# Router softmax on one core: fewer filler matmuls late, late copies out of PSUM shared with ScalarE, the last row loaded in two pieces, and the first store held back

## The chip, the cores and the metric

The kernel runs on one core of one Trainium2 chip. The metric is the device time of one execution in microseconds (us). The kernel before takes 91.72 us, the median of three runs (91.64 to 91.76). The profiled execution took 91.54 us, and its trace spans 89.8 us; the times of the trace count from the start of that span.

## The reference

```python
x: (16, 512, 1024) float32, router_weights: (1024, 8) float32

def reference(x, router_weights):
    logits = np.matmul(x, router_weights)
    exp_logits = np.exp(logits - np.max(logits, axis=-1, keepdims=True))
    return (exp_logits / np.sum(exp_logits, axis=-1, keepdims=True)).astype(np.float32)
```

There are 8192 tokens of 1024 values each. Each is multiplied by a thin 1024x8 matrix, and a softmax over the 8 results follows. The input is 33.6 MB, the output 0.26 MB.

## The kernel before

**Tiling.** Token 64p + j belongs to partition p, so the 8192 tokens are 64 "rows" j of 128 tokens, one for each partition (J = 64). The list `LOADS` says how many rows each transfer brings: thirteen loads of 4 rows, three of 2 and six of 1. The first 4 rows come as float32 on SyncE's queue and are cast by ScalarE (L72). All others are issued by GpSimd (L74), whose queue casts float32 to bfloat16 on the way. All tiles of x stay in SBUF, so no load waits for a buffer of x. GpSimd issues them in order, each from the ninth on after an earlier load has landed.

**A row.** A matmul needs the 1024 values of a token along the partitions, and they lie along the free axis. So TensorE transposes a row in eight 128x128 pieces against an identity matrix into one PSUM tile `pt` (`turn`, L147 to L149; the pool has 4 such tiles[...]). VectorE copies the tile to SBUF as `xT` (L156). Then eight matmuls with 8 columns each accumulate the row's logits (`project`, L98 to L109) into a PSUM tile `lg` of the row's group. The program order on TensorE is written out by hand (a manual schedule): the transposes of row j, then the projection of row j - 2, then fillers.

**Fillers.** `fill(n)` issues n matmuls of 512 columns on constant data into a PSUM tile that nobody reads (L95). They only keep TensorE active. From row 24 to row 61 there are two for each row (L162, L163).

**Softmax.** `GROUPS` puts the rows into seven groups of 8, one of 7 and one of 1. When a group's last row is projected, five steps go into the list `later`: the maximum (`peak`), the subtraction on VectorE and exp on ScalarE (`power`), the sum (`total`), the reciprocal (`recip`), and the scaling into the output tile `outv` (`scale`, L138). The loop over rows pops one step after each row's copy (L157, L158), so they run between the copies on VectorE.

**The end.** The loop covers rows 0 to 62 (L151). After it come the projections of rows 61 and 62 (L166, L167), two softmax steps of the group of 7, and then row 63: four transposes and a copy of 512 columns, twice (L174 to L176), its projection, two more steps, the maximum (L182), an exp that also adds up the row (L185), the last step of the group of 7, a reciprocal (L188) and a scaling (L189). Two stores go out on SyncE's queue: rows 0 to 55 right after group 6 is scaled (L143), and rows 56 to 63 at the very end (L191).

Of the kernel before, what the change touches and what calls it, by code (L numbers as in the profile page):

```python
# [9 lines left out]
@with_exitstack  # L10
def kernel(
    ctx: ExitStack,
    tc: tile.TileContext,
    x: bass.AP,
    router_weights: bass.AP,
    out: bass.AP,
):
    nc = tc.nc
    P = 128
    B, S, D = x.shape  # L20
    D2, N = router_weights.shape
    assert D2 == D
    M = B * S
    KO = D // P
    J = M // P


    x_rows = x.rearrange("b s d -> (b s) d").rearrange("(p j) d -> p j d", p=P)
    out_rows = out.rearrange("b s n -> (b s) n").rearrange("(p j) n -> p j n", p=P)

    fp32 = mybir.dt.float32
    bf16 = mybir.dt.bfloat16
    Exp = mybir.ActivationFunctionType.Exp
    X = mybir.AxisListType.X
    ALU = mybir.AluOpType


    LOADS = [4] * 13 + [2, 2, 2] + [1] * 6
    GROUPS = [8] * 7 + [7, 1]
    assert sum(LOADS) == J and sum(GROUPS) == J  # L40
    STORES = {6: (0, 56), 8: (56, J)}

    const = ctx.enter_context(tc.tile_pool(name="const", bufs=1))
    xpool = ctx.enter_context(tc.tile_pool(name="x", bufs=1))
    xtp = ctx.enter_context(tc.tile_pool(name="xT", bufs=5))
    sm = ctx.enter_context(tc.tile_pool(name="sm", bufs=2))
    psum_t = ctx.enter_context(tc.tile_pool(name="psum_t", bufs=4, space=bass.MemoryType.PSUM))
    psum_f = ctx.enter_context(tc.tile_pool(name="psum_f", bufs=1, space=bass.MemoryType.PSUM))
    psum_l = ctx.enter_context(tc.tile_pool(name="psum_l", bufs=2, space=bass.MemoryType.PSUM))

    x_of = []
    with tc.manual_schedule():
        identity = const.tile([P, P], bf16)
        ident = const.tile([P, P], fp32)
        w8 = const.tile([KO, P, N], fp32)
        w_bf = const.tile([P, KO, N], bf16)
        outv = const.tile([P, J, N], fp32)
        filler = const.tile([P, 512], bf16)


        x_f32 = const.tile([P, LOADS[0], D], fp32)
        for k in range(0, LOADS[0], 2):
            nc.sync.dma_start(out=x_f32[:, k:k + 2, :], in_=x_rows[:, k:k + 2, :])
        nc.scalar.dma_start(
            out=w8[:], in_=router_weights.rearrange("(ko ki) n -> ko ki n", ko=KO)
        )
        j0 = 0
        for i, r in enumerate(LOADS):
            xb = xpool.tile([P, r, D], bf16, name=f"x_{i}", tag=f"x_{i}")
            if i == 0:  # L70
                for k in range(r):
                    nc.scalar.copy(xb[:, k, :], x_f32[:, k, :])  # L72
            else:
                nc.gpsimd.dma_start(out=xb[:], in_=x_rows[:, j0:j0 + r, :])  # L74
            x_of += [(xb, k) for k in range(r)]
            j0 += r
            if i == 2:
                make_identity(nc, ident)
                nc.gpsimd.memset(filler[:], 0.5)  # L79
        nc.vector.tensor_copy(out=identity[:], in_=ident[:])  # L80
        w_ps = psum_l.tile([P, 8, N], fp32, name="lg")
        for n in range(N):
            nc.tensor.transpose(w_ps[:, n, :], w8[:, :, n], ident[0:KO, 0:KO])  # L83
        nc.vector.tensor_copy(out=w_bf[:], in_=w_ps[:].rearrange("p n ko -> p ko n"))  # L84

        group_of = [(g, k) for g, n in enumerate(GROUPS) for k in range(n)]
        first = [sum(GROUPS[:g]) for g in range(len(GROUPS))]
        logits = {}
        pend = []
        later = []  # L90
        spare = psum_f.tile([P, 512], fp32)

        def fill(n):
            for _ in range(n):
                nc.tensor.matmul(spare[:], lhsT=filler[:, 0:P], rhs=filler[:], start=True, stop=True)  # L95


        def project(j, xT):  # L98
            g, k = group_of[j]
            if k == 0:  # L100
                logits[g] = psum_l.tile([P, 8, N], fp32, name="lg")
            for ko in range(KO):
                nc.tensor.matmul(  # L103
                    logits[g][:, k, :],
                    lhsT=xT[:, ko, :],
                    rhs=w_bf[:, ko, :],
                    start=(ko == 0),
                    stop=(ko == KO - 1),
                )  # L109
            if k == GROUPS[g] - 1 and g < len(GROUPS) - 1:  # L110
                softmax(g)

        def softmax(g):
            n, a = GROUPS[g], first[g]
            lg = logits.pop(g)[:, 0:n, :]
            mx = sm.tile([P, n, 1], fp32, name="mx")
            ex = sm.tile([P, n, N], fp32, name="ex")
            ev = sm.tile([P, n, N], fp32, name="ev")
            ssum = sm.tile([P, n, 1], fp32, name="ssum")
            inv = sm.tile([P, n, 1], fp32, name="inv")  # L120

            def peak():
                nc.vector.reduce_max(mx[:, :, 0], lg, axis=X)  # L123

            def power():
                nc.vector.tensor_tensor(  # L126
                    out=ex[:], in0=lg, in1=mx[:].broadcast_to([P, n, N]), op=ALU.subtract
                )
                nc.scalar.activation(ev[:], ex[:], func=Exp)  # L129

            def total():
                nc.vector.reduce_sum(ssum[:, :, 0], ev[:], axis=X)  # L132

            def recip():
                nc.vector.reciprocal(inv[:], ssum[:])  # L135

            def scale():
                nc.vector.tensor_tensor(  # L138
                    out=outv[:, a:a + n, :], in0=ev[:], in1=inv[:].broadcast_to([P, n, N]), op=ALU.mult
                )  # L140
                if g in STORES:
                    lo, hi = STORES[g]
                    nc.sync.dma_start(out=out_rows[:, lo:hi, :], in_=outv[:, lo:hi, :])  # L143

            later.extend([peak, power, total, recip, scale])

        def turn(pt, xb, kos):  # L147
            for ko in kos:
                nc.tensor.transpose(pt[:, ko, :], xb[:, ko * P:(ko + 1) * P], identity[:])  # L149

        for j in range(J - 1):  # L151
            xb, k = x_of[j]
            pt = psum_t.tile([P, KO, P], bf16, name="pt")
            turn(pt, xb[:, k, :], range(KO))
            xT = xtp.tile([P, KO, P], bf16, name="xT")
            nc.vector.tensor_copy(out=xT[:], in_=pt[:])  # L156
            if later:  # L157
                later.pop(0)()  # L158
            pend.append((j, xT))
            if len(pend) > 2:  # L160
                project(*pend.pop(0))
            if 24 <= j < J - 2:  # L162
                fill(2)  # L163


        for p in pend:  # L166
            project(*p)  # L167
        for _ in range(2):
            later.pop(0)()
        xb, k = x_of[J - 1]  # L170
        pt = psum_t.tile([P, KO, P], bf16, name="pt")
        xT = xtp.tile([P, KO, P], bf16, name="xT")
        H = KO // 2
        for kos in (slice(0, H), slice(H, KO)):  # L174
            turn(pt, xb[:, k, :], range(KO)[kos])
            nc.vector.tensor_copy(out=xT[:, kos, :], in_=pt[:, kos, :])  # L176
        project(J - 1, xT)
        for _ in range(2):
            later.pop(0)()
        lg1 = logits.pop(len(GROUPS) - 1)[:, 0, :]  # L180
        low = sm.tile([P, 1], fp32, name="low")
        nc.vector.reduce_max(low[:], lg1, axis=X, negate=True)  # L182
        ev1 = sm.tile([P, N], fp32, name="ev1")
        s1 = sm.tile([P, 1], fp32, name="s1")
        nc.scalar.activation(ev1[:], lg1, func=Exp, bias=low[:], accum_out=s1[:])  # L185
        for step in later:
            step()
        nc.vector.reciprocal(s1[:], s1[:])  # L188
        nc.vector.tensor_scalar_mul(outv[:, J - 1, :], ev1[:], s1[:])  # L189
        lo, hi = STORES[len(GROUPS) - 1]  # L190
        nc.sync.dma_start(out=out_rows[:, lo:hi, :], in_=outv[:, lo:hi, :])  # L191


# [28 lines left out]
```

## Time and profile before

| | before |
|---|---|
| device time, median of 3 | 91.72 us |
| span of the trace | 89.8 us |
| busy: TensorE / VectorE / ScalarE / GpSimd | 65.9 / 50.2 / 7.7 / 12.4 us |
| mean granted TensorE clock | 0.973 of full |
| read from HBM, written | 33.59 MB, 0.26 MB |
| TensorE on transposes (L149) / projections (L103) / fillers (L95) | 43.6 / 22.6 / 22.5 us |
| VectorE on copies out of PSUM (L156) | 43.3 us, 63 copies of 690 ns |
| store of rows 0 to 55: issued, landed after | 84.04 us, 1.9 us |
| store of rows 56 to 63: issued, landed after | 87.42 us, 1.5 us |

The page gives busy time by engine and by group of instructions; the busy times of TensorE's lines overlap, because matmuls are pipelined. The time that a row really takes on TensorE is the distance between the starts of two rows in the timeline. "Landing" is the time from a transfer's issue to the moment at which its completion is seen. Busy shares over the whole span say little here, since the end of the kernel has other limits than its middle; the prediction goes by stretches of the timeline.

### The profile page before, as it was taken

The page shows a single profiled execution, that of the slowest core. Times are in us where ns is not written, and L with a number is a line of the kernel's source. Part 1 is how long each engine was busy: PE and PEld are TensorE (multiplying, and loading weights), DVE is VectorE, ACT ScalarE, POOL GpSimd, SP SyncE. Part 2 cuts the span into 40 slices and gives each one's busy share as a digit, 9 for nine tenths or more (in the row PEclk, how much of TensorE's full clock was granted, in tenths as well). Part 3 has the DMA queues.
Part 4 walks back from the last instruction along what each step waited for, and adds up shares of the span by engine and source line. Part 5 has one row for each costly group of instructions (what it writes and reads, how often), then busy time and mean ns, then how long its engine had stood idle before and what let it go on. Part 6 is the DMA issues. An engine that isn't in the chain of part 4 may idle for free.

```text
span 89.8 us, 2442 instructions
## 1 busy us (share of the span) xinstructions
PE 65.9 (73%) x1108; PEld 54.3 (60%) x1108; DVE 50.2 (56%) x110; ACT 7.7 (9%) x15; POOL 12.4 (14%) x28
## 2 busy tenths in 40 slices
PE   0408008999773819699898989599989999999520
PEld 0406008999663819676775757377757777777410
DVE  0304103669791917657475657457774777677760
ACT  3143035000100010000100010000100010001110
POOL 5990011020202001020202020020202200000000
PEclk9999999999999995799999999999999999999996
DMA  3999999999999999999999999999999999992100
GB/s 58 376 325 281 299 208 219 226 208 215 223 208 215 219 215 212 219 226 201 215 230 201 212 230 204 215 223 219 204 204 217 212 209 205 210 207 47 68 34 15
DMA packets 3625, 18.26 MB, mean 203 GB/s; under 512 B 536, under 2 KB 664, under 8 KB 1824
## 3 DMA queue, kind: packets, MB, share of 16 engines
q0 software_dynamic: 3024, 15.73, 85.4%
q1 hardware_dynamic: 576, 2.36, 6.9%
q8 instruction: 8, 0.13, 0.5%
q10 hardware_dynamic: 16, 0.03, 0.2%
q14 instruction: 1, 0.01, 0.0%
HBM read 33.59 MB, written 0.26 MB: 377 GB/s over the span
## 4 chain that ended last, share of the span: by engine, by line
DMA 70%; PE 18%; DVE 3%; POOL 3%; issue 2%; ACT 0%; ACTq 0%; POOLq 0%
DMA x<-in_x_dram 70%; PE pt L149 8%; PE spare L95 7%; PE lg L103 3%; POOL x L74 2%; DVE xT L176 1%; DVE xT L156 1%; POOL filler L79 1%; POOL ident masks.py:199 0%; ACT ev L185 0%; DVE outv L189 0%; DVE mx L123 0%; POOL ident masks.py:197 0%; DVE ex L126 0%; DVE inv L135 0%
## 5 line engine op out<-in xcount | busy, mean ns | idle before, releaser
L156 DVE COPY xT<-pt 128x1024 bf16<-128x1024 bf16 x63 | 43.3, 690 | 32.4 <-PE pt L149 32.4
L149 PE MATMUL pt<-identity,x 128*128 128x128 bf16 x512 | 43.6, 234 | 16.5 <-DMA x<-in_x_dram 8.1
L149 PEld LDWEIGHTS <-x 128*128 128x128 bf16 x512 | 34.9, 104 | 27.9 <-DMA x<-in_x_dram 11.2
L103 PE MATMUL lg<-w_bf,xT 128*128 128x8 bf16 x512 | 22.6, 168 | 0.8 <-DVE xT L176 0.4
L95 PE MATMUL spare<-filler 128*128 128x512 bf16 x76 | 22.5, 376 | 0.0
L103 PEld LDWEIGHTS <-xT 128*128 128x128 bf16 x512 | 20.5, 99 | 1.0 <-DVE xT L176 0.5
L74 POOL DMA_DIRECT2D x<-in_x_dram x21 | 11.3, 544 | 58.0 <-DMA x<-in_x_dram 57.2
L129 ACT ACTIVATE ev<-ex 128x64 f32<-128x64 f32 (+1 forms) x8 | 2.0, 255 | 68.4 <-DVE ex L126 68.4
L72 ACT CAST x<-x_f 128x1024 bf16<-128x1024 f32 x4 | 4.0, 1042 | 8.1 <-DMA x_f<-in_x_dram 8.1
L95 PEld LDWEIGHTS <-filler 128*128 128x128 bf16 x76 | 4.6, 96 | 0.0
L83 PE MATMUL lg<-ident,w 8*128 8x8 f32 x8 | 1.0, 254 | 3.1 <-POOL ident masks.py:199 3.1
L83 PEld LDWEIGHTS lg<-ident,w 8*128 8x128 f32 x8 | 1.0, 198 | 3.1 <-POOL ident masks.py:199 3.1
L80 DVE CAST identity<-ident 128x128 bf16<-128x128 f32 x1 | 0.5, 514 | 3.0 <-POOL ident masks.py:199 3.0
L123 DVE TENSOR_REDUCE mx<-lg 128x8 f32<-128x64 f32 (+1 forms) x8 | 1.7, 215 | 0.3 <-PE lg L103 0.3
L126 DVE TENSOR_TENSOR ex<-lg,mx 128x64 f32<-128x64 f32 (+1 forms) x8 | 1.7, 215 | 0.0
L138 DVE TENSOR_TENSOR outv<-ev,inv 128x64 f32<-128x64 f32 (+1 forms) x8 | 1.7, 214 | 0.0
L132 DVE TENSOR_REDUCE ssum<-ev 128x8 f32<-128x64 f32 (+1 forms) x8 | 1.7, 208 | 0.0
L135 DVE RECIPROCAL inv<-ssum 128x8 f32<-128x8 f32 (+1 forms) x8 | 1.6, 195 | 0.0
L72 ACT ACT_TABLE_LOAD x1 | 1.3, 1283 | 1.4 <-PEq L206 1.4
L176 DVE COPY xT<-pt 128x512 bf16<-128x512 bf16 x2 | 0.8, 420 | 0.5 <-PE pt L149 0.5
L84 DVE CAST w_bf<-lg 128x64 bf16<-128x64 f32 x1 | 0.2, 225 | 0.6 <-PE lg L83 0.6
L79 POOL MEMSET filler<- 128x512 bf16 x1 | 0.5, 520 | 0.0
(11 smaller groups left out, 1.9 us busy)
## 6 DMA issues: line engine op xcount, KB each, us to landing
x<-in_x_dram POOLq DMA_DIRECT2D x12, 1024.0 KB, 35.3
x_f<-in_x_dram SPq DMA_DIRECT2D x2, 1024.0 KB, 8.2
x<-in_x_dram POOLq DMA_DIRECT2D x3, 512.0 KB, 34.0
x<-in_x_dram POOLq DMA_DIRECT2D x6, 256.0 KB, 18.5
out_dram<-outv SPq DMA_DIRECT2D x1, 224.0 KB, 1.9
w<-in_router_weights_dram ACTq DMA_DIRECT2D x1, 32.0 KB
out_dram<-outv SPq DMA_DIRECT2D x1, 32.0 KB, 1.5
```

Source lines behind the costliest of these rows:

```text
L72: nc.scalar.copy(xb[:, k, :], x_f32[:, k, :])
L74: nc.gpsimd.dma_start(out=xb[:], in_=x_rows[:, j0:j0 + r, :])
L83: nc.tensor.transpose(w_ps[:, n, :], w8[:, :, n], ident[0:KO, 0:KO])
L95: nc.tensor.matmul(spare[:], lhsT=filler[:, 0:P], rhs=filler[:], start=True, stop=True)
L103: nc.tensor.matmul(logits[g][:, k, :], lhsT=xT[:, ko, :], rhs=w_bf[:, ko, :], start=(ko == 0), stop=(ko == KO - 1),)
L123: nc.vector.reduce_max(mx[:, :, 0], lg, axis=X)
L126: nc.vector.tensor_tensor(out=ex[:], in0=lg, in1=mx[:].broadcast_to([P, n, N]), op=ALU.subtract)
L129: nc.scalar.activation(ev[:], ex[:], func=Exp)
L132: nc.vector.reduce_sum(ssum[:, :, 0], ev[:], axis=X)
L138: nc.vector.tensor_tensor(out=outv[:, a:a + n, :], in0=ev[:], in1=inv[:].broadcast_to([P, n, N]), op=ALU.mult)
L149: nc.tensor.transpose(pt[:, ko, :], xb[:, ko * P:(ko + 1) * P], identity[:])
L156: nc.vector.tensor_copy(out=xT[:], in_=pt[:])
```

## The change

The change has five parts, all of which act from row 48 on.

- **Fillers.** One for each row instead of two from row 48, and none from row 60 (before: two for each row up to row 61).
- **Copies out of PSUM.** From row 54 (`NEAR`) a row is transposed into two PSUM tiles, of 5 and 3 pieces. VectorE copies the first (640 columns), ScalarE the second (384 columns). From there a row is projected one row later, not two.
- **Last row.** Row 63 is loaded by two transfers, of 768 and 256 columns. The first is copied by VectorE (512) and ScalarE (256), the second by VectorE. TensorE turns both pieces before it projects row 62.
- **Groups.** Groups of 8 up to row 47, then rows 48 to 53, then rows 54 to 61; rows 62 and 63 stand alone. Each of these two has its maximum and its exp, and then one sum, one reciprocal and one scaling serve both. The pool of `lg` tiles has 3 buffers instead of 2.
- **Stores.** Rows 0 to 53 are stored first, rows 54 to 63 last. Ahead of the first store SyncE issues a transfer of two elements out of the 768-column piece of row 63 into a tile `mark` that nobody reads. SyncE waits for that piece before it issues this transfer, and so the store behind it starts only when x is nearly all there.

```diff
-    LOADS = [4] * 13 + [2, 2, 2] + [1] * 6
-    GROUPS = [8] * 7 + [7, 1]
-    STORES = {6: (0, 56), 8: (56, J)}
+    LOADS = [4] * 13 + [2, 2, 2] + [1] * 5
+    LAST_LOADS = [6, 2]
+    GROUPS = [8] * 6 + [6, 8, 1, 1]
+    DONE = sum(GROUPS[:7])
+    NEAR = 54
-    psum_l = ctx.enter_context(tc.tile_pool(name="psum_l", bufs=2, ...))
+    psum_l = ctx.enter_context(tc.tile_pool(name="psum_l", bufs=3, ...))
+        for i, n in enumerate(LAST_LOADS):
+            xb = xpool.tile([P, n * P], bf16, name=f"xe_{i}", tag=f"xe_{i}")
+            nc.gpsimd.dma_start(out=xb[:], in_=x_rows[:, J - 1, k0 * P:(k0 + n) * P])
...
+        def turn(xb, split, k0=0):
+            pts, i = [], 0
+            for copy, n in zip((nc.vector.tensor_copy, nc.scalar.copy), split):
+                if n:
+                    pt = psum_t.tile([P, KO, P], bf16, name="pt")
...
-        for j in range(J - 1):
-            nc.vector.tensor_copy(out=xT[:], in_=pt[:])
-            if len(pend) > 2:
-            if 24 <= j < J - 2:
-                fill(2)
+        for j in range(J - 2):
+            parts = evict(turn(xb[:, k, :], (KO, 0) if j < NEAR else (5, 3)))
+            while len(pend) > (2 if j < NEAR else 1):
+            if 24 <= j < J - 4:
+                fill(2 if j < 48 else 1)
+        nc.sync.dma_start(out=mark[:], in_=x_last[0][0][0:1, 0:2])
+        nc.sync.dma_start(out=out_rows[:, 0:DONE, :], in_=outv[:, 0:DONE, :])
+        while pend:
+            project(*pend.pop(0))
+        step(2)
+        before = evict(turn(xb[:, k, :], (5, 3)))            # row 62
+        step(1)
+        turned = turn(xa, (4, 2), ka) + turn(xb, (2, 0), kb) # row 63
+        project(J - 2, before)
+        last = evict(turned)
+        step(1)
+        project(J - 1, last)
+        for k in range(2):
+            nc.vector.reduce_max(low[:, k:k + 1], lg, axis=X, negate=True)
+            nc.scalar.activation(ev[:, k, :], lg, func=Exp, bias=low[:, k:k + 1])
+        step(1)
+        nc.vector.reduce_sum(ssum[:, :, 0], ev[:], axis=X)
+        nc.vector.reciprocal(ssum[:], ssum[:])
+        nc.vector.tensor_tensor(out=outv[:, J - 2:J, :], in0=ev[:], in1=ssum[:]..., op=ALU.mult)
+        nc.sync.dma_start(out=out_rows[:, DONE:J, :], in_=outv[:, DONE:J, :])
```

## The prediction

> **What bounds the kernel now.** I read the chain of waits first, to see which resource carries the end, and then the stretches of the last 10 us.
>
> The chain that ended last, in order of time (start, length, what):
>
> ```profile
> 28.58 38.78 DMA x<-in_x_dram
> 67.36 0.05 issue
> 67.41 0.62 PE pt L149 x8
> 68.03 0.18 PE lg L103 x8
> 68.21 0.45 PE spare L95 x2
> ...
> 82.70 0.46 PE pt L149 x8
> 83.16 0.02 issue
> 83.18 0.70 DVE xT L156
> ```
>
> Until 67.4 us the chain is the loading of x. From there TensorE never waits: each row is 0.45 of transposes, 0.18 of projection and 0.45 of fillers, 1.08 us, up to row 62. So the fillers, which compute nothing, are on the path for the last 16 us. The stretches of the span (length, busy time of PE, PEld, DVE, ACT, POOL, clock, DMA share, GB/s) show that the transfers are done before that work:
>
> ```profile
> 80.00:81.00 1.00, 1.00 (x21) 0.76 (x18) 0.77 (x2) 0.14 (x1) 0.00 (x0) 1.00 0.94 180
> 81.00:82.00 1.00, 1.00 (x21) 0.76 (x18) 0.82 (x2) 0.12 (x1) 0.00 (x0) 1.00 0.48 84
> 82.00:83.00 1.00, 1.00 (x21) 0.76 (x19) 0.80 (x2) 0.00 (x0) 0.00 (x0) 1.00 0.00 0
> ```
>
> The tile view of x, restricted to one issue at a time, gives each load's landing. The last row's:
>
> ```profile
> L74 POOL DMA_DIRECT2D x<-in_x_dram x1: 530/530/530, 70.2 to 70.2; - x1
> DMA to landing us min/median/max: 12.2/12.2/12.2
> ```
>
> Issued at 70.16, landed at 82.4. In the same way (issue plus landing) rows 48-51 land at 67.4, 52-53 at 69.9, 54-55 at 72.3, 56-57 at 74.9, and rows 58 to 62 at 76.2, 77.3, 78.5, 79.8 and 81.2: about 1.22 us a row with the DMA engines busy throughout, so x cannot be there sooner. TensorE begins row n at 67.41 + 1.08 (n - 48): row 62 at 82.5, 1.4 us after it landed. Row 63 waits behind row 62's copy and projection and begins at 84.15, 1.75 us late. Its timeline:
>
> ```profile
> 84.15 0.38 PE L149 MATMUL pt<-identity,x 128*128 128x128 bf16 x4
> ...
> 85.60 0.42 DVE L176 COPY xT<-pt 128x512 bf16<-128x512 bf16 x1 [0.47 <-PE pt L149]
> ...
> 86.08 0.26 PE L103 MATMUL lg<-w_bf,xT 128*128 128x8 bf16 x4 [0.44 <-DVE xT L176]
> ...
> 86.57 0.27 ACT L185 ACTIVATE ev<-lg,low 128x8 f32<-128x8 f32 x1 [1.44 <-DVE low L182]
> ...
> 87.42 0.34 SPq L191 DMA_DIRECT2D out_dram<-outv  x1
> ```
>
> From this last issue to the end of the span are 89.8 - 87.42 = 2.4 us, which the change cannot shorten. The floor by x is thus 82.4 plus a tail; today the store is issued 5.0 us after x is complete.
>
> [...] the clock is 0.50 from 33.6 to 37.0, and the eight transposes of a row take 1.01 us there, not 0.61. [...]
>
> **The change part by part.**
>
> *Fillers.* A filler is 0.45 / 2 = 0.225 us on the chain. Rows 48 to 59 lose one each, rows 60 and 61 two each: 16 x 0.225 = 3.6 us of TensorE time. A row costs 0.86 us with one and 0.63 with none, both under the 1.22 us in which a row lands. So TensorE catches up: from 67.41, rows 48-51 take until 70.9, 52-53 until 72.6, 54-55 until about 74.4. VectorE, with 0.69 a copy and 0.21 for a softmax step, copies row 53 by 73.2 and row 55 by about 74.6. Rows 56-57 land at 74.9: from there every row is turned as it lands. The 3.6 us are not all gained, since the transfer takes over as the bound; the gain is the lateness of 1.75 us at row 63 plus what the tail saves.
>
> *Shared copies.* VectorE copies cost 0.42 us for 512 and 0.69 for 1024 columns, so 0.53 ns a column: 0.49 for 640 and 0.285 for 256. For ScalarE no copy out of PSUM is in the trace; its cast of 1024 columns takes 1.04 and its exp of 64 takes 0.255, so 0.82 ns a column: 0.52 for 384 and 0.41 for 256. Its exp from PSUM (0.27 for 8 columns) against exp from SBUF bounds an extra for PSUM at about 0.07, so 0.52 to 0.6. A row is ready 0.2 us sooner than with one copy. For rows 54 to 61 this hides under the 1.22 us a row. There is one activation table load in the whole trace, ahead of a cast, and exp later needs no other, so I charge none.
>
> *Last row.* The pieces have a 3/4 and 1/4 share of 1.22 us. [...] I take 0.05 (0 if only bytes count, 0.3 if a quarter-row costs half a row). So the second piece lands at 82.45 and the first at 82.15.
>
> *The tail, step by step.* Row 62 lands at 81.2, is turned behind row 61's projection, and its ScalarE copy comes behind the exp of rows 54 to 61 (about 81.85 to 82.1), so it ends near 82.6. The first piece: TensorE 82.15; four transposes to the start of the copy 0.42 (85.18 to 85.60 before); VectorE 82.57 to 82.99. ScalarE's 256 columns: 82.7 to 83.1. The second piece: TensorE 82.5 behind six transposes, two transposes 0.31, but VectorE is busy; a copy starts 0.08 before its predecessor's recorded end (85.94 against 86.02 before), so 82.91 to 83.2. Row 62's projection (0.35) and two softmax instructions lie beside that. Last two projection matmuls at 83.25, 0.21 (four took 0.26), 83.46; maximum 83.48 to 83.65; exp 83.67 to 83.94; sum 83.97, 0.20; reciprocal 84.19, 0.17; scaling 84.38, 0.21; store issued at 84.6. The sum is new (0.22), in place of reading the accumulator (0.12 after exp): costs 0.1. Row 62's softmax hides beside row 63. Against 87.42 that is 2.8 us sooner: 1.75 of lateness, and 1.05 from the shorter tail (before, from row 63's first transpose to the store 3.27 us; now 2.1 from the second piece).
>
> *Stores.* The added wait stands on SyncE's queue, with only the first store and the last one behind it. It ends at 82.15; the tiny transfer's issue takes 0.35, the store's 0.35, so it is issued at 82.5. Before, its bytes moved about 0.9 to 1.9 us after its issue (192 GB/s between 85 and 86); now 83.4 to 84.4, before the last store's, issued at 84.6. 40 KB there instead of 32 cost nothing I can see. Without the wait the store could go near 79, amid the loads.
>
> *lg buffers and groups.* A third buffer lets rows 62 and 63 have their own tiles; no instruction of the path before waits for one. Nothing.
>
> **Sum.** 91.72 - 2.8 = 88.9 us.
>
> **The rivals.**
> - *The clock falls late.* With fewer fillers TensorE is busy 0.63 of 1.22 us, 52%, for rows 60 to 62. Before, the clock fell after the 3.4 us from 30.2 to 33.6, with 1.25 us busy (37%), and not after the 3.4 us ahead, with 1.83 (54%). [...] If it falls, [...] eight for row 63 add 0.43, projections and latencies about 0.2: 89.5.
> - *The two engines trip over each other at the end.* ScalarE holds two copies and three exps in the last 1.8 us, VectorE a row of eleven instructions. One more wait for the exp of rows 54 to 61, or a late second piece (+0.3), costs 0.5 to 1: 89.6.
> - *The transfer is hidden anyway, no gain.* It would need the end to hang on something with a fixed end, such as the held store. For it the last store would have to land behind the first by 2.8 us; the traffic above ends at 84.4. Time 91.7.
> - *Slower.* The clock falls at row 48 and stays. A row in the cold stretch is 1.07 us, plus 0.45 for a filler: 12 x 1.52 + 3 x 1.07 = 21.5, so row 63 starts at 88.9, and a tail of 2.7 gives 91.6 against 87.42: 95.9. Against it: TensorE is then busy all the time, and the trace shows full clock again after 3.4 us.
>
> **How the numbers follow.** Forecast 0.72, clock 0.12, trip 0.11, no gain 0.02, slower 0.03. The forecast's own errors (0.3 for landing, 0.08 a ScalarE copy, some 0.03 for each of ten handovers) spread it from 88.4 to 89.4; the two near rivals reach 90.1, which I take as the top, and 88.3 as the bottom. Only the last two cases lie outside on purpose, and what is left is for steps I missed. Faster 0.95, same 0.02, slower 0.03.
>
> **What would show it.** In the profile after: TensorE idle before rows 56 to 63 with x's transfer as the releaser; the second piece landing at 82.4 to 82.5; ScalarE copies of 384 columns near 0.52; the sum of rows 62 and 63 near 84.0; the last store issued at 84.6; clock 1.00 between 78 and 84. A clock under 1 there, a wait of VectorE for ScalarE, or a first store still moving after 85.4 would make it wrong.

## The result, and the profile after

The changed kernel takes 88.91 us (median of 4 runs, 88.74 to 89.18) against 91.68 us for the kernel before (4 runs, 91.57 to 91.76). The ratio is 0.970, with a 95% interval of 0.967 to 0.973. The forecast was 88.9 us.

The chain of waits of the kernel after, in order of time (start, length, what):

```profile
33.68 36.30 DMA x<-in_x_dram
69.98 0.28 issue
70.27 11.84 DMA xe<-in_x_dram
82.11 0.05 issue
82.16 0.41 PE pt L162 x4
82.57 0.02 issue
82.59 0.43 DVE xT L173
83.03 0.05 issue
83.07 0.42 PE lg L114 x8
```

Before, the chain left the loading of x at 67.4 us and ran over TensorE for 16 us. Now it stays with the loading until 82.1 us, when the first piece of row 63 lands. No filler (L104) is on it any more. The page's list of transfers gives the landings (issue plus landing time): the first piece 70.27 + 11.8 = 82.1, the second 72.72 + 9.7 = 82.4. Row 63 landed at 82.4 before, too. The loading has not become faster; the kernel now ends sooner after it.

The same stretches as before (length, busy PE, PEld, DVE, ACT, POOL, clock, DMA share, GB/s):

```profile
80.00:81.00 1.00, 0.77 (x16) 0.68 (x16) 0.49 (x1) 0.32 (x1) 0.00 (x0) 1.00 1.07 180
81.00:82.00 1.00, 0.91 (x16) 0.71 (x16) 0.48 (x3) 0.16 (x1) 0.00 (x0) 1.00 0.65 101
82.00:83.00 1.00, 0.82 (x16) 0.72 (x16) 0.92 (x4) 0.92 (x3) 0.00 (x0) 1.00 0.03 4
```

TensorE was busy all of the time between 80 and 83 us; now it has gaps, and ScalarE works beside VectorE. The last steps in the timeline of after:

```profile
82.16 0.64 PE L162 MATMUL pt<-identity,xe 128*128 128x128 bf16 x8 [0.24 <-DMA xe<-in_x_dram]
82.17 0.91 ACT L173 COPY xT<-pt 128x384 bf16<-128x384 bf16 x2
...
82.59 0.62 DVE L173 COPY xT<-pt 128x512 bf16<-128x512 bf16 x2
...
83.51 0.17 DVE L214 TENSOR_REDUCE low<-lg 128x1 f32<-128x8 f32 x1 [0.16 <-PE lg L114]
...
84.02 0.17 DVE L219 TENSOR_REDUCE ssum_last<-ev_last 128x2 f32<-128x16 f32 x1 [0.20 <-ACT ev_last L215]
...
84.62 0.34 SPq L224 DMA_DIRECT2D out_dram<-outv  x1
```

TensorE waits 0.24 us for x before it turns row 63. The eight transposes of both pieces run without a gap, and VectorE's two copies (512, then 256 columns) stand one behind the other. The last store is issued at 84.62, not 87.42, and the span ends 2.4 us later, at 87.0, as it did before. So the span is 2.8 us shorter, all of it ahead of the last store.

### The profile page after: what moved, and what is told of

Same layout as the page of the kernel before. It is cut to its first block, busy times and chain, and to the rows that moved or that the text cites. A ratio compares the mean times of both kernels' runs of the same rounds, so it can differ in the third digit from the quotient of the medians.

```text
span 87.0 us, 2427 instructions
## 1 busy us (share of the span) xinstructions
PE 63.8 (73%) x1092; PEld 53.6 (62%) x1092; DVE 48.1 (55%) x112; ACT 12.4 (14%) x25; POOL 12.9 (15%) x29
## 3 DMA queue, kind: packets, MB, share of 16 engines
q0 software_dynamic: 3168, 15.73, 88.3%
## 4 chain that ended last, share of the span: by engine, by line
DMA 89%; POOL 3%; issue 2%; DVE 1%; PE 1%; ACT 0%; POOLq 0%
DMA x<-in_x_dram 75%; DMA xe<-in_x_dram 14%; POOL x L76 2%; POOL filler L81 1%; DVE xT L173 0%; PE lg L114 0%; PE pt L162 0%; POOL ident masks.py:199 0%; ACT ev_last L215 0%; POOL ident masks.py:197 0%; DVE ssum_last L219 0%; DVE low L214 0%; DVE ssum_last L220 0%; DVE outv L221 0%; POOLq L239 0%
## 5 line engine op out<-in xcount | busy, mean ns | idle before, releaser
L173 DVE COPY xT<-pt 128x1024 bf16<-128x1024 bf16 (+2 forms) x65 | 42.0, 652 | 31.8 <-PE pt L162 31.6
L104 PE MATMUL spare<-filler 128*128 128x512 bf16 x60 | 19.2, 384 | 0.0
L76 POOL DMA_DIRECT2D x<-in_x_dram x20 | 10.7, 543 | 56.2 <-DMA x<-in_x_dram 55.4
L173 ACT COPY xT<-pt 128x384 bf16<-128x384 bf16 (+1 forms) x10 | 4.7, 467 | 5.1 <-PE pt L162 4.9
L104 PEld LDWEIGHTS <-filler 128*128 128x128 bf16 x60 | 4.1, 96 | 0.0
L86 POOL DMA_DIRECT2D xe<-in_x_dram x2 | 1.1, 527 | 3.9 <-DMA x<-in_x_dram 3.9
L162 PE MATMUL pt<-identity,xe 128*128 128x128 bf16 x8 | 0.6, 222 | 0.2 <-DMA xe<-in_x_dram 0.2
## 6 DMA issues: line engine op xcount, KB each, us to landing
xe<-in_x_dram POOLq DMA_DIRECT2D x1, 192.0 KB, 11.8
```

Of the source, the lines that this page charges most:

```text
L162: nc.tensor.transpose(pt[:, c, :], xb[:, (i + c) * P:(i + c + 1) * P], identity[:])
L173: copy(out=xT[:], in_=pt[:, 0:n, :])
```

## The experiments

My theory was the one of the prediction: x's landing is the floor, the fillers kept TensorE away from it, and the other parts shorten what comes after x. The rivals were that the fillers are all of the gain, that they are none of it, or that the held store carries it. The medians below come from three groups of runs, each with its own runs of the kernel before (91.85, 91.70 and 91.63 us). So I compare gains, each against the kernel before of the same group. The changed kernel, run again in the third group, gains 91.63 - 88.83 = 2.80 us; that is the measure for all others. The three medians of the kernel before differ by up to 0.2 us, so I read nothing into differences of gains under some 0.2 us.

**Only the fillers thinned.** The kernel before, with one edit:

```diff
-            if 24 <= j < J - 2:
-                fill(2)
+            if 24 <= j < J - 4:
+                fill(2 if j < 48 else 1)
```

> The kernel before with only the fillers thinned as in the change. Theory (x's transfer is the floor; fillers made TensorE 1.4 to 1.75 us late): row 62 is turned as it lands at 81.2, its whole copy on VectorE ends near 82.55, row 63 starts near 82.8 and not 84.15, so 1.35 us is gained: 90.3 us. Rival A (fillers are all of it): 88.9 us like the whole change. Rival B (the other parts bring the gain, fillers were hidden): 91.7 us.

Measured: 90.49 us (90.19 to 91.19), a gain of 1.36 us, ratio 0.986 (0.984 to 0.989). Both rivals fall: the fillers are about half of it. The timeline of this kernel shows what holds it there:

```profile
81.96 0.69 DVE L156 COPY xT<-pt 128x1024 bf16<-128x1024 bf16 x1 [0.44 <-PE pt L149]
...
82.71 0.36 PE L103 MATMUL lg<-w_bf,xT 128*128 128x8 bf16 x8 [0.40 <-DVE xT L156]
...
82.92 0.38 PE L149 MATMUL pt<-identity,x 128*128 128x128 bf16 x4
...
83.95 0.58 PE L149 MATMUL pt<-identity,x 128*128 128x128 bf16 x4 [0.64 <-DVE xT L176]
...
86.41 0.34 SPq L191 DMA_DIRECT2D out_dram<-outv  x1
```

Row 63 is turned at 82.92, no longer at 84.15, yet x, which had landed at 82.6 (70.36 + 12.2), is not what TensorE waits for there. It waits for VectorE's copy of row 62 and projects row 62 first. The fillers were not the only thing ahead of row 63.

Something else took back part of the gain. TensorE's clock fell to half at 83.3 in this profile, and the second four transposes of row 63 took 0.58 us, against 0.38 for the first four and for the same four in the kernel before. From row 63's first transpose to the last store this kernel takes 3.49 us, the kernel before 3.27. So with the clock up the gain might have been near 1.6 us; that is an estimate from this one profile.

**The fillers put back.** The changed kernel with the old two lines, `if 24 <= j < J - 2: fill(2)`.

> The changed kernel with two fillers a row up to row 61 again. Theory: TensorE is late again, row 62 is turned near 82.8 and the second piece of row 63 near 83.6 instead of 82.5: 90.0 us, with the shorter tail kept. Rival A (fillers are all of it): 91.7 us. Rival B (the other parts bring the gain): 88.9 us.

Measured: 90.48 us (90.33 to 90.59), a gain of 1.37 us, ratio 0.986 (0.984 to 0.987). The fillers are thus worth 2.80 - 1.37 = 1.43 us in the changed kernel and 1.36 in the old one, there with the fallen clock; the gains of the two halves, 1.36 and 1.37, add up to nearly the whole. My figure of 90.0 was 0.5 too low. Row 62 is turned at 83.29, not at 82.8, and the second piece of row 63 at 84.40, not at 83.6. A part of the second delay is a wait that I had left out. The chain of this kernel shows it:

```profile
83.73 0.23 DVE ex L137
83.95 0.41 DVE xT L173
84.40 0.27 PE pt L162 x2
84.67 0.63 PE lg L114 x16
```

Rows 62 and 63 take five PSUM tiles, and the pool has four. When TensorE is late, both pieces of row 63 lie ready at once, and the second piece has to wait until VectorE has emptied row 62's tile; TensorE stands still for 0.17 us. In the changed kernel that tile is free by the time the second piece has landed, and the eight transposes run on without a gap.

**The store not held.** The changed kernel without the tiny transfer:

```diff
-        mark = const.tile([1, 2], bf16)
-        nc.sync.dma_start(out=mark[:], in_=x_last[0][0][0:1, 0:2])
         nc.sync.dma_start(out=out_rows[:, 0:DONE, :], in_=outv[:, 0:DONE, :])
```

> The changed kernel without the tiny transfer that holds the first store. Theory: the store of 216 KB goes out near 79 among the last loads, takes 0.5 to 1.0 us of DMA time from them, and the last piece lands later by some 0.6 us: 89.5 us. Rival (the hold is idle, the loads win or the store fits in): 88.9 us. Rival (the hold carries most of the gain): above 90.3 us.

Measured: 88.95 us (88.78 to 89.00), a gain of 2.90 us, ratio 0.969 (0.967 to 0.970). The hold gains nothing that can be measured, and my 89.5 was wrong. The tile view of `outv` around 79 us shows the store that was let go:

```profile
L193 SPq DMA_DIRECT2D out_dram<-outv x1: 348/348/348, 78.8 to 78.8; - x1
...
DMA to landing us min/median/max: 4.4/4.4/4.4
```

It went out at 78.8, among the loads, as I had expected. But it landed after 4.4 us; the held store of the same size takes 1.9. The stretches of this kernel show where more bytes moved than in the changed kernel (the last column is GB/s):

```profile
80.50:81.00 0.50, 0.43 (x13) 0.34 (x10) 0.38 (x1) 0.16 (x1) 0.00 (x0) 1.00 1.18 196
81.00:81.50 0.50, 0.33 (x9) 0.32 (x10) 0.11 (x1) 0.32 (x1) 0.00 (x0) 1.00 1.12 279
81.50:82.00 0.50, 0.50 (x11) 0.40 (x9) 0.32 (x2) 0.00 (x0) 0.00 (x0) 1.00 0.71 125
82.00:82.50 0.50, 0.24 (x5) 0.17 (x4) 0.50 (x3) 0.34 (x2) 0.00 (x0) 1.00 0.54 187
```

With the hold, the same four stretches move 165, 124, 78 and 7 GB/s, and up to 80.5 the two kernels' rates are alike (192 and 195 just before). The excess is (31 + 155 + 47 + 180) x 0.5 us = 206 KB, nearly the whole store. A total rate does not tell whose bytes moved, but the packets in the trace do: the store's first one starts at 80.84, 2.0 us after the issue (0.86 us with the hold), and its last one ends at 82.85. So its bytes moved at the end of the loads, while the share of the DMA engines that the loads took was falling. In this profile the second piece landed at 72.7 + 10.0 = 82.7, 0.3 us later than with the hold; but row 60, which landed just as the store was issued, was already 0.3 us later (78.9 against 78.6), so that delay is not the store's. Why the store started so late was not tested.

**One load for the last row.** `LAST_LOADS = [8]`, and row 63 turned 5 + 3 like row 62.

> The changed kernel with row 63 in one load of 1024 columns, turned 5 + 3 like row 62. Theory: the row lands at 82.4, ScalarE's part of it is copied by 83.6, the maximum starts near 83.9 instead of 83.5: 89.3 us. Rival (the split is hidden or costs as much in short runs as it saves): 88.9 us.

Measured: 89.45 us (89.35 to 89.65), a gain of 2.40 us. The split is worth 0.4 us. In this kernel's timeline row 63 is turned at 82.61, ScalarE copies its 384 columns from 83.33 to 83.81, and the maximum starts at 84.13; with the split it starts at 83.51.

**No ScalarE copies.** Every row `(KO, 0)`, and row 63 in copies of 768 and 256 columns on VectorE.

> The changed kernel with all copies out of PSUM on VectorE (whole rows; row 63 in copies of 768 and 256 columns). Theory: row 62's whole copy and row 63's 768 columns stand one behind the other on VectorE, its last copy ends near 83.5 and not 83.2, the maximum starts near 83.8: 89.2 us. Rival (ScalarE's share is hidden behind the loads even in the last two rows): 88.9 us. Rival (ScalarE's share is the larger part of what the tail gained): 90.0 us or more.

Measured: 89.27 us (89.02 to 89.72), a gain of 2.43 us; ScalarE's share is worth 0.37. The timeline of this kernel around row 63:

```profile
82.22 0.69 DVE L173 COPY xT<-pt 128x1024 bf16<-128x1024 bf16 x1
...
82.95 0.74 DVE L173 COPY xT<-pt 128x768 bf16<-128x768 bf16 x2
...
84.00 0.17 DVE L214 TENSOR_REDUCE low<-lg 128x1 f32<-128x8 f32 x1 [0.16 <-PE lg L114]
```

Row 62's whole copy keeps VectorE until 82.9, and row 63's two copies follow until 83.7, 0.5 us later than in the changed kernel (83.2).

**Row 62 projected first.** Of the 1.37 us that are not the fillers', the split and ScalarE account for 0.77, and the hold for nothing. What was left in the code was above all the order on TensorE:

```diff
-        turned = turn(xa, (4, 2), ka) + turn(xb, (2, 0), kb)
         project(J - 2, before)
+        turned = turn(xa, (4, 2), ka) + turn(xb, (2, 0), kb)
```

> The changed kernel with row 62 projected before row 63's pieces are turned, as the kernel before does it. The split load takes 0.54 us, ScalarE's copies 0.35 and the hold nothing off the end, so some 0.5 us of the tail's gain of 1.4 is still without a cause. Theory: it is this order; row 63 waits for row 62's last copy (ScalarE, 82.6), its first piece is turned at 82.8 and not 82.16, the last store goes out 0.6 us later: 89.5 us. Rival (the common end of rows 62 and 63 or the regrouping brings it): 88.9 us.

Measured: 89.36 us median (89.31 to 89.99), a gain of 2.27 us. The order is worth 0.53 us, as expected. Two of the five runs took 89.87 and 89.99, the others 89.31 to 89.36. The profiled execution is not the median one but the one of 89.99 us. Two things in it are unlike the changed kernel's profile. Row 62 landed at 67.70 + 14.0 = 81.7 and not at 81.2, so it was turned at 81.76 and not at 81.31. And the clock fell:

```profile
79.77:83.18 3.41, 2.24 (x42) 1.86 (x43) 1.55 (x5) 1.21 (x4) 0.00 (x0) 1.00 0.55 91
...
83.20:84.60 1.40, 1.31 (x18) 1.04 (x14) 0.86 (x4) 0.38 (x2) 0.00 (x0) 0.50 0.42 158
```

TensorE's clock (the third number from the right) fell to half at 83.2, while row 63 was being turned. From row 63's first transpose to the start of the maximum this run takes 84.73 - 83.10 = 1.63 us, the changed kernel 83.51 - 82.16 = 1.35. So some 0.3 us, by this estimate, go to the clock, and the rest of the 0.63 us above the median to the late row. Whether the other long run has the same causes was not seen, since only one was profiled. In the changed kernel's second profile row 62 was late too (turned at 81.64), and the last store went out at 84.69, only 0.07 us later than in the first: with row 63 turned first, a late row 62 hardly counts. The fallen clock is the first rival of the prediction. It is seen in two of these kernels, here and with only the fillers thinned, at a price of 0.2 to 0.3 us.

**No fillers from row 48, and none at all.** In the changed kernel `if 24 <= j < 48: fill(2)`, and then no `fill` call at all.

> The changed kernel with no filler from row 48 on. Theory (x's transfer bounds these rows, TensorE has slack): 88.9 us, the same within 0.3. Rival (the fillers keep the clock up for the last rows): [...] 89.5 us, with a clock of 0.5 between 78 and 83 us. Rival (every filler taken away gains time): 88.5 us or less.

> The changed kernel with no filler at all. Theory: a row takes 1.07 us on TensorE even at half clock, less than the 1.22 us in which it lands, so the clock before row 62 costs nothing; if it is at half in the last two rows the tail grows by 0.4 to 0.6: between 88.9 and 89.5 us, 89.3 taken. Rival (fillers hold the kernel's speed): above 90.5 us. Rival (fillers never matter once few enough): 88.9 us with full clock at the end.

Measured: 88.95 us (88.88 to 89.18), a gain of 2.75, without the late ones, and 88.74 us (88.65 to 88.79), a gain of 2.96, without any. So the fillers that the change left add nothing, and those from row 48 on cost nothing that can be told from the runs' scatter. Without any the kernel is 0.2 us faster than without the late ones, in the same group and with no overlap of their runs; the runs do not show why. My 89.3 for no fillers was wrong: the clock was up again before the last rows. The rows of the page for that kernel (40 slices of the span; busy share and clock in tenths):

```profile
PE   0318005999296896639691886979797996685730
...
PEclk9999999999975569995799755555558999999999
```

and its stretches before and in the tail:

```profile
49.00:66.00 17.00, 15.03 (x225) 14.77 (x223) 10.65 (x24) 0.52 (x2) 1.58 (x3) 0.50 1.02 214
...
78.00:84.00 6.00, 3.98 (x82) 3.31 (x79) 3.58 (x14) 2.96 (x8) 0.00 (x0) 1.00 0.70 133
```

From 49 to 66 us TensorE worked at half clock, at 1.07 us a row, and still kept up with x at 1.22. From 78 to 84 us the clock was full. In the kernel without the late fillers it was at half from 74.9 to 78.3 us, and full after that. In both, half clock cost nothing where it stood; it cost time where it met row 63, in the two runs above.

**A version a little ahead of both.** No fillers, and row 63's sum taken by the exp itself:

```diff
+            acc = {"accum_out": ssum[:, 1, :]} if k else {}
-            nc.scalar.activation(ev[:, k, :], lg, func=Exp, bias=low[:, k:k + 1])
+            nc.scalar.activation(ev[:, k, :], lg, func=Exp, bias=low[:, k:k + 1], **acc)
...
-        nc.vector.reduce_sum(ssum[:, :, 0], ev[:], axis=X)
+        nc.vector.reduce_sum(ssum[:, 0, :], ev[:, 0, :], axis=X)
```

> The changed kernel once more, on the chip of the next two kernels, for comparison: 88.9 us.

> The changed kernel with no filler at all, and with row 63's sum taken by the exp itself on ScalarE, so that only row 62's sum is a VectorE instruction and lies beside it. Theory: from the exp's start to the reciprocal 0.39 as in the kernel before, not 0.50, so 0.1 us sooner: 88.7 us (88.8 if fillers cost nothing at all). Rival (ScalarE's reading of the accumulator costs what the sum cost): 88.8 to 88.9 us.

Measured on one chip: 88.83 us (88.77 to 88.85) for the changed kernel and 88.64 us (88.54 to 88.77) for this one, ratios to the kernel before of 0.970 (0.968 to 0.971) and 0.968 (0.967 to 0.969). The fastest runs of the one and the slowest of the other touch, so a gain of some 0.2 us is likely rather than sure. How much of it is the fillers and how much the sum, these runs do not part; each against the kernel before of its own group, the kernel without fillers alone gains 2.96 us and this one 2.99. In the timeline the maximum starts at 83.38 and the store is issued at 84.38, 1.00 us later; in the changed kernel 83.51 and 84.62, 1.11.

## Why the prediction was right, point by point

**Floor by x.** Right. The second piece landed at 82.4 (forecast 82.45), the first at 82.1 (82.15); the 0.05 us in both forecasts was a guess of mine, taken from no trace. Rows from 60 on are turned as they land, with TensorE waiting 0.47 us for row 61. The forecast had this from row 56 on; rows 57 to 59 were still turned back to back, 0.86 us apart, which cost nothing.

**Tail.** Right almost to the instruction: maximum 83.51 (83.48), sum 84.02 (83.97), store 84.62 (84.6), and 2.4 us from there to the end. Two terms were mis-sized without effect. ScalarE's copy of 384 columns took 0.48 us, less than the 0.52 to 0.6 that I took from its cast and exp. And the tiny transfer's issue took 0.70 us and not 0.35, so the first store went out at 82.88; SyncE had until 84.62.

**Where the gain comes from.** The sum was right and its division was not. I booked 1.75 us as lateness that the fillers caused and 1.05 as the shorter tail. Undoing one thing at a time, against 2.80 in all:

| part undone | gain left, us | worth of the part, us |
|---|---|---|
| fillers thinned | 1.37 | 1.43 |
| row 63 turned before row 62 is projected | 2.27 | 0.53 |
| row 63 in two loads | 2.40 | 0.40 |
| ScalarE copies | 2.43 | 0.37 |
| store held | 2.90 | none (-0.10) |

The worths sum to 2.63. The new groups and the common end of rows 62 and 63 were not undone alone; the sum leaves 0.17 us for them, which is no more than the groups of runs differ by. The step that failed is "the gain is the lateness of 1.75 us at row 63 plus what the tail saves", in the paragraph on fillers: the fillers measured 1.43 and not 1.75, since part of that lateness was not TensorE's load but the order, in which row 63 stood behind row 62's copy and projection. The first experiment shows it, with row 63 at 82.92 while x was there at 82.6. What was not the fillers' is 1.37 and not 1.05.

**The store.** The prediction said that without the wait the store "could go near 79, amid the loads". It did, but that cost nothing: the kernel gained 2.90 us, and 2.80 with the store held. That the store would take 0.5 to 1.0 us from the loads was a guess of mine that no trace had shown; in the one before no store runs beside the loads. Here its first packet moved only 2.0 us after the issue, it landed after 4.4 us, and the kernel was no slower.

**The clock.** From two stretches of the kernel before, one 37% busy with a fall after it and one 54% busy with none, I had estimated that the clock falls below a busy share between the two. That does not hold. In the changed kernel it fell at 24.3 us after 3.41 us with 1.92 busy, which is 56%, in the run with row 62 projected first after 2.24 of 3.41, which is 66%, and with only the fillers thinned after 2.40 of 3.41, which is 70%. The 52% that I booked for the late rows was wrong too: from 78.9 to 82.3 us the changed kernel's TensorE was busy for 2.46 of 3.41, which is 72%. The forecast that the clock stays up in the changed kernel held in both profiles of it, but not for the reason given; that much was luck.

In the profile of the changed kernel the clock changes at 24.3, 27.7, 34.5, 41.4 and, after TensorE's work, at 85.7 us; in that of the kernel before at 33.6, 37.0 and 88.3. Within each of the two these moments lie 3.41 us or a whole multiple of it apart, but not across the two (24.3 + 3 x 3.41 = 34.5, not 33.6). With row 62 projected first the clock fell at 83.2, in the first experiment at 83.3. So an execution of the changed kernel that was not profiled may have met a fall at row 63. The price that I gave a fall in the tail, 0.6 us, was too high: the two that were seen cost 0.2 and 0.3 us by the estimates above, one of them with all but the start of row 63 turned at half clock. I had put down 0.43 us of it to row 63's eight transposes; they took 0.99 us there and 0.64 in the changed kernel, 0.35 more. For the case in which the clock stays at half, I relied on the kernel before, where it was back after 3.4 us at half in which TensorE was busy without a gap (33.6 to 37.0). The kernel without fillers stayed at half clock for 17 us with TensorE busy for 88% of them.

**The rivals.** The two that end near 89.5 were not seen in either profile of the changed kernel, and those without gain or slower had no support in any run.

## What to carry to other kernels

Find when the last input lands, and list what stands between that moment and the last store: useful work queued ahead of it, in the order of the program, cost time here (0.53 us) just as needless work did (1.43 us). When an engine is late by some time, do not book all of it to the needless work on that engine; remove that work alone and see what the next wait is. TensorE at half clock cost nothing here while it still kept up with the loads (1.07 us a row against 1.22), so filler work has to pay at the end of the kernel, if anywhere.

## What the runs showed of the hardware that I had not expected

- A store issued beside running loads was put off: its first packet started 2.0 us after the issue, not 0.86, and its 216 KB landed in 4.4 us, not 1.9. The kernel gained as much as with the store held (2.90 against 2.80 us).
- TensorE's clock stayed at half from 49 to 66 us with TensorE busy 15.03 of 17.0 us, and came back near 66 us, after a stretch in which TensorE was busy without a gap:

```profile
59.50:62.90 3.40, 2.95 (x48) 2.86 (x46) 2.41 (x6) 0.00 (x0) 0.00 (x0) 0.50 1.02 212
62.90:66.30 3.40, 3.40 (x54) 3.40 (x53) 2.03 (x6) 0.26 (x1) 0.53 (x1) 0.53 0.99 206
```

Four stretches of 3.41 us with 2.85 to 2.99 us busy, from 49.0 to 62.7 us, did not bring the clock back. In the changed kernel it came back at 41.4 us after such a stretch with 3.06 us busy. What decides it was not shown.
- VectorE was not slowed by ScalarE when both emptied PSUM: 640 columns took VectorE 0.49 us with ScalarE's 384 (0.48 us) beside it, just what VectorE's copies alone had led me to expect, and 512 columns took 423 ns beside ScalarE's copies and 420 in the kernel before. The forecast took that for granted; the trace before has no ScalarE copy out of PSUM. The two read different tiles. A ScalarE copy without VectorE beside it was not measured.
